# Neighbourhood attention in a two-network kernel: the values' products of two pairs of heads back to back, the context's output products spread, the decay levels one step ahead, own tiles at the end

## The chip, the cores and the metric

The kernel runs on one core of one Trainium2 chip. The metric is the device time of one execution in microseconds (us); lower is better. The kernel before took 1268.24 us, the median of three runs (1267.25 to 1268.48).

The engines are named as in the profile: PE is the matrix engine (TensorE; PEld its loading of weights), DVE the vector engine, ACT the scalar engine, POOL GpSimd, and SP the engine that starts most DMA transfers. PE reads its operands from SBUF and writes into PSUM, which has eight banks here; DVE and ACT read the products from there. Each engine runs its own instructions in the order in which they were written for it, and waits at a semaphore when an operand, or the place for a result, isn't there yet.

## The reference, cut to what matters

Two blocks of layers follow each other on 256 tokens of 1024 numbers. Everything is float32.

```python
def gla_mixer(h, w_in, w_gk_up, b_gk, g_onorm, w_out):      # gated linear attention
    proj = h @ w_in                                          # q, k, v, r, gk_low
    log_a = log_sigmoid(gk_low @ w_gk_up + b_gk) / 16
    ...
    # per chunk of 64 tokens, b = cumsum(log_a):
    decay = exp(where(causal, b_i - b_j, -inf))
    attn = einsum('bhik,bhjk,bhijk->bhij', qb, kb, decay)
    state = state * exp(b_last) + k_dec.T @ vb
    ...
    return (rms_norm(o, g_onorm) * silu(r)) @ w_out

x = x + gla_mixer(rms_norm(x, ...), ...)
x = x + sqrelu_mlp(rms_norm(x, ...), w1, w2)
x = rms_norm(x, final_norm)
# second block: 256 latent tokens (h) and 256 context tokens (hc)
# layer 0, neighbourhood attention: 16 heads of 64, a window of 8 rows x 16 columns, bias rpb
y_lat = softmax([q k_nb * scale + bias, q k_ctx * scale]) @ [v_nb, v_ctx] @ w_o
y_ctx = softmax(q_ctx k_ctx * scale) @ v_ctx @ w_o
# then a SwiGLU FFN on both, grouped-query attention with rotary angles, a second FFN
return rms_norm_2(h, norm_final)
```

## The kernel before, in words

One function, `net`, writes the whole program. A float32 product is made of three products of a narrower float type (`mm3`, lines 178 to 180): high part times high part, low times high, and high times low. So every weight tile of 128 x 1024 that SP loads (`w_load`, line 150) is split by ACT into a high part `wh` (line 161) and by DVE into the rest `wl` (line 162). `wnext` hands out the tiles in one fixed order (`UNITS`) and splits a few ahead (`cap`). The tiles `wh` and `wl` lie in a ring of 12; the probabilities of the neighbourhood attention use the same ring.

The order of the instructions of PE, POOL and SP, and of DVE in most places, comes from a scheduler that works at build time on the program as it is written; ACT's order is the written one in the parts below, and at the end DVE's as well (`manual_schedule`). All 8 PSUM banks are tiles of one pool.

**Gated linear attention (lines 425 to 680).** Eight units `f` make q and k, transposed. Then a loop over `k` makes the values `v`: 12 products of 512 columns for each `k` (two tiles of tokens, two halves, three products; `mm_r`). Two sets of gate products (`gate_half`) follow. Beside them the matrix of decayed scores is built by levels. `decay_sums(t)` (line 431) makes the cumulated log decay of token tile `t` with four products against a triangle, and ACT copies it out (line 433). Then there are nine generators, `core`: `level_diag` (products line 488, masked by DVE on line 490), seven times `level` (subtractions by DVE on lines 501 and 502, exponentials by ACT on line 504, multiplications by DVE on lines 507 and 508, then eight products on PE, line 522, or line 516 for the last level, and a masked copy by DVE, line 528), and `level_cross` (products line 545). `core_step()` runs the products of the generator that stands open and opens the next one, which writes its part on DVE and ACT up to the products. It is called once after each `k`. So a level's DVE work is written one `k` ahead of its products.

`heads_out` and `gated_heads` (line 621) make the outputs of the heads, `heads_T(ks)` transposes them (PE line 630; ACT copies the high part, line 633, DVE makes the low part, line 634). The loop over `w_out` (line 662) does three of its eight `k` for both token tiles, and keeps the last five in `late`; these follow tile by tile, so that the first token tile is done early. Ahead of the last unit of the second tile, `to_T` (line 217) transposes the first tile for the next layer: eight transposes, evacuated by ACT (line 224) and DVE (line 225).

**Neighbourhood attention (lines 821 to 1059).** There are eight pairs of heads, and for each pair six units of work (two heads, and for each the context's queries and two tiles of latent queries). `staged` starts a unit per step and moves every unit that is under way by one stage: scores on PE (lines 891 and 892, 922 and 923), the maximum on DVE, the exponential on ACT (lines 900, 932 and 933), the division on DVE (lines 905 and 937), four transposes on PE (lines 911 and 941), the copy by ACT (lines 915 and 945). In each step `fill(n)` puts some of the generator `steps` between them: the projections of the next pairs (`na_proj`; ACT lines 862 to 878, DVE lines 864 to 876), and at the end the context's output products (`oproj_ctx`, 16 steps of three products). After the last unit of a pair, `done` hands over `na_pv` (line 948), the products of probabilities and values: 24 products into one bank (line 957), those of the two heads side by side in halves of the array; in the step after that ACT copies (line 963) and DVE subtracts (line 964) to make `oT`, which the output products read.

**The end (lines 1493 to 1543).** The last products come in three pieces: 512 columns, 256 and 256. After each, DVE adds the residual (lines 1499 and 1500), ACT squares and sums (line 1502), and DVE multiplies by the gain (line 1535), in place, so behind ACT's reading of the same tile. Then DVE adds the sums (line 1536), POOL makes the root (line 1538), ACT scales the second half (line 1539) and DVE the first (line 1541), and two DMAs write them out.

## Time and profile before

| | before |
|---|---|
| median of three runs | 1268.24 us |
| the profiled execution: its own time | 1267.33 us |
| its span in the trace | 1265.5 us |
| granted clock of PE | 0.998 |
| PE busy | 1249.0 us, 99% of the span |
| DVE busy | 920.0 us, 73% |
| ACT busy | 686.1 us, 54% |
| POOL busy | 79.2 us, 6% |
| DMA, mean rate | 183 GB/s |

The span is the time from the first to the last instruction of the profiled execution; its own time holds the starting and ending around that. Rows of the timeline give the start in us, the duration in us, engine, line, operation, and the names of what is written and read; a number in square brackets is the time for which the engine stood idle before the row, with the instruction whose end it waited for. The matrix engine works in a pipeline, so a product's duration is longer than the distance to the next one's start. That distance, from start to start, tells what a product costs PE.

### The profile page before, as it was taken

What the parts mean: (1) busy time and instruction counts of PE and PEld (TensorE: products, weight loads), DVE (VectorE), ACT (ScalarE), POOL (GpSimd) and SP (SyncE); (2) the same over time, 40 slices, a digit from 0 to 9 for tenths busy, and PEclk for the clock granted to TensorE, in tenths of its full rate; (3) what the DMA queues carried; (4) which work ended last, traced back from release to release, by engine and by line L of the source; (5) the groups of instructions that cost most, each with busy time, mean ns of one, the idle gap of its engine ahead of it and who ended that gap; (6) DMA issues with size and microseconds to landing.
All of it is one profiled execution on the core that took longest, in us unless ns stands there. A gap on an engine that the chain in (4) does not pass through costs nothing.

```text
span 1265.5 us, 18648 instructions
## 1 busy us (share of the span) xinstructions
PE 1249.0 (99%) x6874; PEld 1043.6 (82%) x6874; DVE 920.0 (73%) x1629; ACT 686.1 (54%) x1335; POOL 79.2 (6%) x139
## 2 busy tenths in 40 slices
PE   9999999999999999999999999999999999999997
PEld 8878898988888777789888888888888677899996
DVE  5868788797988888777877667623668888655555
ACT  7565655666548888754332122323457797644443
POOL 1000000030100000001000000000002320000000
PEclk9999999999999999999999999999999999999999
DMA  8646587877572334463656777633664224665650
GB/s 302 202 133 212 190 293 255 283 267 260 183 251 98 126 114 114 155 197 114 210 184 204 248 258 252 219 100 102 198 200 117 67 84 128 215 190 184 187 180 34
DMA packets 68507, 231.22 MB, mean 183 GB/s; under 512 B 8048, under 2 KB 8736, under 8 KB 68416
## 3 DMA queue, kind: packets, MB, share of 16 engines
q1 hardware_dynamic: 68128, 229.68, 56.0%
q8 instruction: 54, 0.88, 0.3%
q10 hardware_dynamic: 288, 0.35, 0.1%
q14 instruction: 37, 0.30, 0.1%
HBM read 228.93 MB, written 1.07 MB: 182 GB/s over the span
## 4 chain that ended last, share of the span: by engine, by line
PE 84%; DVE 7%; ACT 6%; issue 1%; DMA 1%; POOL 0%; POOLq 0%; SPq 0%; DVEq 0%; ACTq 0%
PE b L178 26%; PE b L179 25%; PE b L180 25%; DVE wl L162 2%; PE b L1420 1%; ACT wh L161 1%; PE b L217 1%; PE b L1406 1%; PE b L522 1%; DMA raw<-in_wst_dram 1%; DVE a L309 1%; ACT t L878 1%; DVE t L309 1%; PE b L1387 0%; PE b L957 0%
## 5 line engine op out<-in xcount | busy, mean ns | idle before, releaser
L161 ACT CAST wh<-raw 128x1024 fp32r<-128x1024 f32 x310 | 322.8, 1044 | 391.2 <-PE b L179 295.7
L162 DVE TENSOR_TENSOR wl<-raw,wh 128x1024 fp32r<-128x1024 f32 x310 | 375.0, 1215 | 157.7 <-ACT wh L161 154.0
L179 PE MATMUL b<-t,wl 128*128 128x256 f32 (+1 forms) x1120 | 365.8, 327 | 0.3 <-DVE wl L162 0.3
L178 PE MATMUL b<-t,wh 128*128 128x256 f32 (+1 forms) x1120 | 366.1, 327 | 0.0
L180 PE MATMUL b<-t,wh 128*128 128x256 f32 (+1 forms) x1120 | 365.3, 327 | 0.0
L178 PE MATMUL b<-wh,t 128*128 128x512 f32 (+1 forms) x748 | 298.2, 401 | 1.2 <-ACT t L235 0.6
L180 PE MATMUL b<-wl,t 128*128 128x512 f32 (+1 forms) x748 | 295.1, 395 | 0.0
L179 PE MATMUL b<-wh,t 128*128 128x512 f32 (+1 forms) x748 | 294.9, 394 | 0.1
L179 PEld LDWEIGHTS b<-t,wl 128*128 128x128 f32 x1120 | 210.8, 188 | 22.6 <-DVE wl L162 0.6
L178 PEld LDWEIGHTS b<-t,wh 128*128 128x128 f32 x1120 | 210.7, 188 | 22.3 <-issue 0.2
L180 PEld LDWEIGHTS b<-t,wh 128*128 128x128 f32 x1120 | 210.5, 188 | 20.6 <-DVE t L236 0.2
L180 PEld LDWEIGHTS b<-wl,t 128*128 128x128 f32 x748 | 140.5, 188 | 33.7
L178 PEld LDWEIGHTS b<-wh,t 128*128 128x128 f32 x748 | 140.4, 188 | 32.6 <-ACT t L235 1.0
L179 PEld LDWEIGHTS b<-wh,t 128*128 128x128 f32 x748 | 140.8, 188 | 31.0 <-DVE t L634 0.6
L309 DVE CUSTOM_DVE_ANT_0 a<-a,crow 128x1024 f32<-128x1024 f32 x96 | 117.0, 1226 | 28.3 <-DMA a<-in_ada_dram 27.7
L309 DVE CUSTOM_DVE_ANT_0 t<-a,crow 128x1024 bf16<-128x1024 f32 x64 | 78.5, 1236 | 8.8 <-DMA a<-in_ada_dram 8.8
L1065 DVE TENSOR_TENSOR t<-b,t 128x512 f32<-128x512 f32 (+1 forms) x42 | 23.6, 563 | 59.4 <-PE b L180 52.2
L190 POOL TENSOR_TENSOR c<-c,mhalf 128x1 f32<-128x1 f32 x21 | 14.2, 674 | 537.7 <-DVE c L189 537.6
L324 POOL TENSOR_TENSOR mod<-mod,bcol 128x8 f32<-128x8 f32 x20 | 14.4, 719 | 478.3 <-DVE mod L309 476.0
L1071 ACT CAST t<-t 128x512 fp32r<-128x512 f32 (+1 forms) x42 | 21.7, 517 | 34.6 <-DVE t L1065 34.6
L197 ACT ACTIVATE t<-t 128x512 f32<-128x512 f32 x40 | 24.8, 624 | 10.8 <-DVE t L1034 6.4
L1396 ACT ACTIVATE t<-b,c,c 128x512 f32<-128x512 f32 x32 | 25.9, 811 | 3.4 <-POOL c L1394 3.4
(239 smaller groups left out, 1201.4 us busy)
## 6 DMA issues: line engine op xcount, KB each, us to landing
raw<-in_wst_dram SPq DMA_DIRECT2D x310, 512.0 KB, 4.4
a<-in_ada_dram SPq DMA_DIRECT2D x96, 512.0 KB, 4.4
t<-in_rpb_dram SPq DMA_DIRECT2D x16, 256.0 KB, 4.1
t<-row SPq DMA_DIRECT2D x12, 256.0 KB, 4.9
t<-in_ctx_dram SPq DMA_DIRECT2D x8, 256.0 KB, 5.8
t<-in_xt_dram SPq DMA_DIRECT2D x4, 256.0 KB, 5.9
t<-in_x_dram SPq DMA_DIRECT2D x4, 256.0 KB, 6.3
crow<-in_cvec_dram SPq DMA_DIRECT2D x2, 512.0 KB
```

What stands on the lines that cost most here:

```text
L161: A.copy(out=h[:, :n], in_=raw[:, :n])
L162: V.tensor_tensor(out=l[:, :n], in0=raw[:, :n], in1=h[:, :n], op=ALU.subtract)
L178: T.matmul(o, lhsT=lh, rhs=rh, start=first, stop=False)
L179: T.matmul(o, lhsT=ll, rhs=rh, start=False, stop=False)
L180: T.matmul(o, lhsT=lh, rhs=rl, start=False, stop=last)
L190: G.tensor_tensor(out=ms[:, 3:4], in0=ms[:, 2:3], in1=mhalf[:, 0:1], op=ALU.pow)
L197: A.activation(out=junk[hf], in_=halves[hf], func=AF.Square, scale=1.0 / 32.0, accum_out=ms[:, hf:hf + 1])
L309: V.tensor_tensor_reduce(out=raw if ci == n_c - 1 else t2([D], BF16), in0=raw, in1=crow[ci], scale=1.0, scalar=0.0, op0=ALU.mult, op1=ALU.add,
L324: G.tensor_tensor(out=m, in0=m, in1=bcol[:, L, v, :], op=ALU.add)
L1065: V.tensor_tensor(out=a, in0=pg_[:, :n], in1=a, op=ALU.mult)
L1071: A.copy(out=h, in_=a)
L1396: A.activation(out=pl, in_=sl, func=AF.Exp, scale=r, bias=mx[:, 1:2], accum_out=mx[:, 2:3])
```

## The change

It has five parts.

1. `decay_sums(0)` and `decay_sums(1)` come after units 6 and 7 of the `f` loop (before: after unit 7, and after `k` = 0 of the value loop). `level_diag` and the first `level` are opened ahead of the value loop, so two generators stand open all the time: a level's products come one `k` earlier, and its DVE work is written two `k` ahead of them.
2. The `w_out` loop does four `k` at once and keeps four (before: three and five). Transposes 4 and 5 of `heads_T` come after `k` = 1, 6 and 7 after `k` = 2 (before: all four after the loop).
3. The eight transposes of the first token tile come in three lots, 2, 3 and 3, around the last three units of the second tile (before: all eight ahead of the last unit).
4. `na_pv` takes a list of pairs. Pairs (0, 1), (2, 3) and (4, 5) have their products done one group after the other, each group in its own bank; pairs 6 and 7 stay alone. From unit 40 on `fill` takes one and two steps in turn, up to unit 52 (before: two, up to unit 47).
5. At the end the products with the gain go to tiles of their own, `ys_`; the product of the first half with the gain moves ahead of the last piece; and the last DVE instruction is a product with one scalar (before: with the scalar and with the gain).

```diff
-        if f == 7:
-            decay_sums(0)
+        if f > 5:
+            decay_sums(f - 6)
...
+    for _ in range(2):
+        open_.append(core.pop(0))
+        run(open_[-1])
...
-        if k == 0:
-            decay_sums(1)
...
-        if k < KD - 5:
+        if k < KD - 4:
             for t in range(NT):
                 mm_r(ac[t], u, yT[k], t, k == 0, False)
         else:
             late.append((k, u))
-    heads_T(range(4, KD))
+        if k in (1, 2):
+            heads_T((2 * k + 2, 2 * k + 3))
     hT = new_T()
+    first_T = to_T_steps([xin[0]], hT, 0, vc[:, V_FFN0, :])
     for t in range(NT):
         for k, u in late:
-            if (t, k) == (1, KD - 1):
-                to_T([xin[0]], hT, 0, vc[:, V_FFN0, :])
+            if t == 1 and k > KD - 4:
+                run(first_T, k - KD + 5)
             mm_r(ac[t], u, yT[k], t, False, k == KD - 1)
         residual(xin[t], ac[t])
+    run(first_T, KD)
...
-    def na_pv(pr):
-        po = bank()
+    def na_pv(prs):
+
+        pos = []
+        for pr in prs:
+            po = bank()
...
+            pos.append(po)
+        yield
+        for pr, po in zip(prs, pos):
+            oT[pr] = (t2([N2], F32R), t2([N2], F32R))
+            A.copy(out=oT[pr][0], in_=po)
+            V.tensor_tensor(out=oT[pr][1], in0=po, in1=oT[pr][0], op=ALU.subtract)
...
     def fill(n):
-        if n < len(order):
-            run(steps, (n + 1) * 16 // 6 - n * 16 // 6 if n < 40 else 2)
+        if n < len(order) + 5:
+            run(steps, (n + 1) * 16 // 6 - n * 16 // 6 if n < 40 else 1 + n % 2)
...
     def done(m):
         pr, r = divmod(m, 6)
-        return [na_pv(pr)] if r == 5 else []
+        if r < 5 or pr in (0, 2, 4):
+            return []
+        return [na_pv((pr - 1, pr) if pr < 6 else (pr,))]
...
-    ms, zs_ = col(), [t2([512]) for _ in range(2)]
+    ms, zs_, ys_ = col(), [t2([512]) for _ in range(2)], [t2([512]) for _ in range(2)]
...
-        if n > 0:
-            V.tensor_tensor(out=zs_[1][:, lo:lo + w], in0=zs_[1][:, lo:lo + w], in1=nfb[1][:, lo:lo + w], op=ALU.mult)
+        for y, z, g in ((ys_[1][:, lo:lo + w], zs_[1][:, lo:lo + w], nfb[1][:, lo:lo + w]), (ys_[0], zs_[0], nfb[0]))[:(0, 2, 1)[n]]:
+            V.tensor_tensor(out=y, in0=z, in1=g, op=ALU.mult)
...
-    A.activation(out=zs_[1], in_=zs_[1], func=AF.Copy, scale=r)
-    out_rows(nc.scalar, 1, 512, zs_[1])
-    V.scalar_tensor_tensor(out=zs_[0], in0=zs_[0], scalar=r, in1=nfb[0], op0=ALU.mult, op1=ALU.mult)
-    out_rows(nc.sync, 1, 0, zs_[0])
+    A.activation(out=ys_[1], in_=ys_[1], func=AF.Copy, scale=r)
+    out_rows(nc.scalar, 1, 512, ys_[1])
+    V.tensor_scalar(out=ys_[0], in0=ys_[0], scalar1=r, scalar2=None, op0=ALU.mult)
+    out_rows(nc.sync, 1, 0, ys_[0])
```

Where the scheduler puts this shows in the order of the instructions. On PE, at the end of the value loop, the kernel before has the products of the fifth and sixth level (tiles `t_744` and `t_748`, `t_782` and `t_786`) with one product of the weight stream between them; the rows ahead are products of 512 columns.

```order
L178 MATMUL b_514<-wh_632,t_124 128x512
L179 MATMUL b_514<-wh_632,t_124 128x512
L522 MATMUL b_770<-t_744 128x128 x2
L522 MATMUL b_776<-t_744 128x128 x2
L522 MATMUL b_770<-t_748 128x128 x2
L522 MATMUL b_776<-t_748 128x128 x2
L180 MATMUL b_514<-wl_633,t_124 128x512
L522 MATMUL b_806<-t_782 128x128 x2
L522 MATMUL b_813<-t_782 128x128
L522 MATMUL b_806<-t_786 128x128 x2
L522 MATMUL b_813<-t_782 128x128
L522 MATMUL b_813<-t_786 128x128 x2
```

The kernel after has the sixth level's products (tiles `t_738` and `t_742`) behind a whole `k` of the weight stream, 12 products; these are the last seven of them, and the first of the next `k`.

```order
L180 MATMUL b_531<-wl_620,t_123 128x512
L178 MATMUL b_532<-wh_620,t_123 128x512
L179 MATMUL b_532<-wh_620,t_123 128x512
L180 MATMUL b_532<-wl_620,t_123 128x512
L178 MATMUL b_533<-wh_620,t_123 128x512
L179 MATMUL b_533<-wh_620,t_123 128x512
L180 MATMUL b_533<-wl_620,t_123 128x512
L522 MATMUL b_806<-t_738 128x128 x2
L522 MATMUL b_806<-t_742 128x128 x2
L522 MATMUL b_813<-t_738 128x128 x2
L522 MATMUL b_813<-t_742 128x128 x2
L178 MATMUL b_530<-wh_668,t_124 128x512
```

Before, 14 products of the stream stood between the groups of most levels, and one between the last two; after, there are 12 between every two of the six groups, ahead of the first and behind the last.

On PE in the neighbourhood attention, the kernel before goes from a pair's last product with the values (bank `b_4244`) to the next unit's scores (line 922) and the projection of a later pair.

```order
L957 MATMUL b_4244<-p_4091,t_3449 64x256
L957 MATMUL b_4244<-p_4194,t_3449 64x256
L957 MATMUL b_4244<-p_4091,t_3451 64x256
L957 MATMUL b_4244<-p_4194,t_3451 64x256
L922 MATMUL b_4257<-t_3862,t_3860 128x512
L923 MATMUL b_4257<-t_3864,t_3860 128x512
```

The kernel after goes from the same products (line 965 there) to those of the next pair, in the bank `b_4474`.

```order
L965 MATMUL b_4461<-p_4091,t_3449 64x256
L965 MATMUL b_4461<-p_4194,t_3449 64x256
L965 MATMUL b_4461<-p_4091,t_3451 64x256
L965 MATMUL b_4461<-p_4194,t_3451 64x256
L965 MATMUL b_4474<-t_4272,t_3449 64x256
L965 MATMUL b_4474<-t_4380,t_3449 64x256
```

The first of the two groups has moved behind the whole of the next pair; the number of products is the same.

On DVE, the last rows of the kernel before are these; `t_12430` is the second half of the last token tile, `t_12429` the first.

```order
L1499 TENSOR_TENSOR t_12430<-b_12449,t_10540 128x256
L1500 TENSOR_TENSOR t_12430<-t_12430,t_80 128x256
L1535 TENSOR_TENSOR t_12430<-t_12430,t_10543 128x256
L1499 TENSOR_TENSOR t_12430<-b_12469,t_10540 128x256
L1500 TENSOR_TENSOR t_12430<-t_12430,t_80 128x256
L1531 SCALAR_TENSOR_TENSOR c_12428<-c_12428 128x1
L1535 TENSOR_TENSOR t_12430<-t_12430,t_10543 128x256
L1536 TENSOR_TENSOR c_12428<-c_12428 128x1
L1541 SCALAR_TENSOR_TENSOR t_12429<-t_12429,c_12428,t_10542 128x512
```

And these those of the kernel after, whose line numbers are 12 higher.

```order
L1511 TENSOR_TENSOR t_12430<-b_12451,t_10540 128x256
L1512 TENSOR_TENSOR t_12430<-t_12430,t_80 128x256
L1547 TENSOR_TENSOR t_12432<-t_12430,t_10543 128x256
L1547 TENSOR_TENSOR t_12431<-t_12429,t_10542 128x512
L1511 TENSOR_TENSOR t_12430<-b_12472,t_10540 128x256
L1512 TENSOR_TENSOR t_12430<-t_12430,t_80 128x256
L1543 SCALAR_TENSOR_TENSOR c_12428<-c_12428 128x1
L1547 TENSOR_TENSOR t_12432<-t_12430,t_10543 128x256
L1548 TENSOR_TENSOR c_12428<-c_12428 128x1
L1553 TENSOR_SCALAR t_12431<-t_12431,c_12428 128x512
```

One DVE instruction of 512 columns is new, ahead of the last piece, and the products with the gain write `t_12431` and `t_12432`, which ACT's squares don't read.

25 lines of the change are left out of this document (11 added, 14 removed).

## The prediction

> **What bounds the kernel now.** I read the page first, then the list of what PE waited for, then the timeline around those waits, and the table of stretches for the attention.
>
> ```profile
> PE 1249.0 (99%) x6874; PEld 1043.6 (82%) x6874; DVE 920.0 (73%) x1629; ACT 686.1 (54%) x1335; POOL 79.2 (6%) x139
> ```
>
> ```profile
> PE b L522 <- DVE t L508: 1.6, 1, 1.6
> ```
>
> PE is busy for 1249.0 of 1265.5 us, so PE's queue is the path, and nothing here removes a product: the gain can only be time in which PE stands, or goes slower than its pace. The list of waits has one long one, 1.6 us at the levels. Since idle time counts from modelled ends, I go by distances from start to start. The next rows are the timeline: PE, ACT and DVE at the levels, then a stretch of the attention that waits for nothing.
>
> ```profile
> 41.86 1.95 PE L488 MATMUL b<-t,t 128*128 128x128 f32 x16
> ...
> 52.16 1.95 PE L522 MATMUL b<-t 128*128 128x128 f32 x16
> ...
> 57.21 1.95 PE L522 MATMUL b<-t 128*128 128x128 f32 x16
> ...
> 69.25 0.47 PE L180 MATMUL b<-wl,t 128*128 128x512 f32 x1
> 71.28 2.02 PE L522 MATMUL b<-t 128*128 128x128 f32 x16 [1.55 <-DVE t L508]
> ...
> 39.26 0.65 ACT L433 COPY t<-b 128x256 f32<-128x256 f32 x2 [1.38 <-PE b L431]
> ...
> 40.87 1.28 ACT L504 ACT_TABLE_LOAD   x1
> ...
> 44.45 0.42 DVE L501 TENSOR_TENSOR t<-t 128x256 f32<-128x256 f32 x1
> ...
> 47.81 1.22 DVE L162 TENSOR_TENSOR wl<-raw,wh 128x1024 fp32r<-128x1024 f32 x1
> 48.94 1.35 DVE L528 COPY_PREDICATED t<-masks,b 128x512 f32<-128x512 uint8 x2
> ...
> 54.00 1.34 DVE L528 COPY_PREDICATED t<-masks,b 128x512 f32<-128x512 uint8 x2
> ...
> 520.27 0.60 PE L911 MATMUL b<-cm,t 128*128 128x128 f32 x4
> 520.63 0.48 PE L178 MATMUL b<-wh,t 128*128 128x512 f32 x1
> 520.95 0.40 PE L179 MATMUL b<-wh,t 128*128 128x512 f32 x1
> 521.18 0.39 PE L180 MATMUL b<-wl,t 128*128 128x512 f32 x1
> ```
>
> The last four rows give the pace: four transposes 0.36, a product of 512 columns behind them 0.32, any other 0.23. DVE's masked copies stand 5.06 apart: that is its round for a level. At 69.25 one product takes 2.03 us.
>
> **Part 1, the levels.** The product at 69.25 should take 0.32, so the wait costs 1.7. What comes in its place? With 12 products between groups instead of 14, PE's round is 5.05 (52.16 to 57.21) less 2 x 0.23 = 4.6; DVE's stays 5.06, so DVE loses 0.5 per level and needs a lead at the start. It gets one: with both sums ahead of the value loop ACT's copies end near 37.1 (39.26 + 0.65 less one `k` of 12 x 0.23 = 2.8), and the first subtraction comes near 36.9 instead of 44.45, no longer behind line 490. From there to the masked copy it was 4.5 us (44.45 to 48.94); the table load, now in the way until 38.4, adds 0.5: 41.9. Then come two maskings (1.2, as line 528) and the second level's arithmetic, a round less masking and split (5.06 - 1.2 - 1.1 = 2.8), and one subtraction more, 0.3: its factors are there at 46.2, and the later levels' 5.06 apart. PE has line 488 at 41.86 - 2.8 = 39.05, the first level 4.6 later, and wants the second's at 48.2. So the lead is 2.0, then 1.5, 1.1, 0.6, 0.1 and about nothing for line 516. I charge 0.1 there: **1.6** (0.9 to 1.8).
>
> **Parts 2 and 3, transposes.** In the timeline of PE:
>
> ```profile
> 118.42 0.40 PE L178 MATMUL b<-wh,t 128*128 128x512 f32 x1
> 118.95 0.50 PE L179 MATMUL b<-wh,t 128*128 128x512 f32 x1
> ...
> 127.87 0.40 PE L180 MATMUL b<-wl,t 128*128 128x512 f32 x1
> 128.64 0.58 PE L217 MATMUL b<-cm,t 128*128 128x128 f32 x2 [0.37 <-DVE t L225]
> 129.16 0.51 PE L178 MATMUL b<-wh,t 128*128 128x512 f32 x1
> ```
>
> At 118.42 a product takes 0.53 instead of 0.23; it stands for DVE's low part of a head's transpose. Transposed one or two `k` earlier, the heads are ready in time; late next is line 621, whose result the new place wants about when it is there: **0.3** (0 to 0.4). At 127.87 the eight transposes run out of banks: 0.77 - 0.23 = 0.54, then 0.52 for two transposes worth 0.2. In lots of 2, 3, 3 with six products between, a lot's evacuations fit between lots: **0.85** (0.5 to 1.0). No load on SP's queue is moved past a wait here; ACT's weight casts stay among the evacuations.
>
> **Part 4, the values' products.** PE again, around one group and around the late places:
>
> ```profile
> 421.42 0.60 PE L911 MATMUL b<-cm,t 128*128 128x128 f32 x4
> 421.95 1.08 PE L957 MATMUL b<-t,t 128*64 128x256 f32 x8
> ...
> 424.69 0.50 PE L922 MATMUL b<-t,t 128*128 128x512 f32 x1
> 425.03 0.39 PE L923 MATMUL b<-t,t 128*128 128x512 f32 x1
> ...
> 504.62 0.47 PE L178 MATMUL b<-wh,t 128*128 128x512 f32 x1
> 505.29 0.38 PE L891 MATMUL b<-t,t 128*128 128x256 f32 x1 [0.19 <-ACT t L900]
> ...
> 521.88 0.39 PE L180 MATMUL b<-wl,t 128*128 128x512 f32 x1
> 522.64 0.63 PE L941 MATMUL b<-cm,t 128*128 128x128 f32 x4 [0.36 <-ACT t L933]
> ...
> 523.58 0.63 PE L941 MATMUL b<-cm,t 128*128 128x128 f32 x4 [0.31 <-ACT t L915]
> ```
>
> Four transposes, the group and the next product take 0.53 + 2.74 + 0.34 = 3.61 (421.42 to 425.03); without the group, 0.68 (520.27 to 520.95). So a group alone costs 2.93. The second of a double group costs its body, 2.74, or some 0.1 less where its first and last pair lose what they lose now by the switch. Three merges at 0.2 to 0.33: **0.9** (0 to 1.0), the low end if the 0.17 on entry is a wait for the probabilities. The Trainium skill speaks to that: "TensorEngine Tiling (Array Packing)", section "Key Properties", says that changing the tiling mode drains the engine. By that rule each merge saves two switches, and the sum stays as it is; without it, it would be 0.5 to 0.9 smaller.
>
> At 504.62 a product takes 0.67 instead of 0.32, since line 891 waits for ACT; ACT has a double group's time there now: **0.35** (0 to 0.35). In the tail, 0.76 instead of 0.23 at 521.88, and 0.94 at 522.64 for four transposes worth 0.4: 1.05 in all. The spread output products go between. I leave 0.2: **0.85** (0.3 to 1.0).
>
> What the merge costs is seen in the table of stretches, one pair each (length, then busy PE, PEld, DVE, ACT), and in the timeline of the second pair.
>
> ```profile
> 402.35:421.95 19.60, 19.60 (x114) 15.49 (x113) 17.29 (x50) 16.27 (x45) 0.00 (x0) 1.00 0.34 111
> 421.95:441.53 19.58, 19.58 (x114) 15.49 (x113) 16.84 (x49) 16.30 (x44) 0.00 (x0) 1.00 0.35 109
> ```
>
> ```profile
> 412.68 0.49 DVE L937 TENSOR_SCALAR t<-t,c 128x512 f32<-128x512 f32 x1
> ...
> 416.11 0.60 PE L941 MATMUL b<-cm,t 128*128 128x128 f32 x4
> ```
>
> A pair without its group is 19.6 - 2.74 = 16.8 us of PE. DVE's 16.84 to 17.29, less 0.7 for line 964, are 16.1 to 16.6: it keeps up only if nearly all its idle time goes. DVE's division ends 2.9 us ahead of its transposes (413.17, 416.11), so a later short pair may lose 2.7 without harm. The first may not: its lead is the 2.74 of the group at 402.35, which goes. I charge 0.4 there, once (0 to 1.5).
>
> **Part 5, the end.** DVE's and ACT's last rows:
>
> ```profile
> 1256.64 0.42 DVE L1500 TENSOR_TENSOR t<-t,t 128x256 f32<-128x256 f32 x1
> ...
> 1258.03 0.42 DVE L1535 TENSOR_TENSOR t<-t,t 128x256 f32<-128x256 f32 x1 [0.97 <-ACT t L1502]
> 1258.38 0.41 DVE L1499 TENSOR_TENSOR t<-b,t 128x256 f32<-128x256 f32 x1
> ...
> 1259.61 0.19 ACT L1502 ACTIVATION_READ_ACCUMULATOR t<-t 128x1 f32 x1
> ...
> 1260.17 0.15 DVE L1536 TENSOR_TENSOR c<-c 128x1 f32<-128x1 f32 x1
> ```
>
> The product with the gain waits 0.97 for ACT, and line 1499 of the last piece stands behind it. Without the wait DVE goes on at 1257.06 with 0.35 for that product and some 0.55 for the new one of 512 columns, and line 1499 starts near 1257.96, 0.42 earlier. Line 1536 then follows ACT's sum at once (1259.80 - 0.42 = 1259.4) and not a product later: **0.76** (0.6 to 0.9). The shorter last instruction lies beside ACT's scaling and its DMA: nothing.
>
> **Sum.** 1.6 + 0.3 + 0.85 + 0.9 + 0.35 + 0.85 + 0.76 = 5.6; less 0.4 for the first short pair and 0.2 for new waits of a tenth each: 5.0. The profiled execution's own time, 1267.33, is 0.9 under the median of 1268.24, within the runs' spread, so the sum is taken from the median: **1263.2 us**, and a profiled execution near 1262.3.
>
> **The rivals.**
>
> *The short pairs are DVE's.* For: 16.1 to 16.6 against 16.8, and ACT and DVE answer each other several times in a unit. Against: the later pairs' leads. If the first loses 1.5 and the other two 0.4 each, 1.9 more than I charged goes: 1265.1. Chance 0.15.
>
> *The pairs keep 19.6 us, and the merge is a loss.* If scores, maximum, exponential, division and copies need 19.6 with the group or without, short pairs save nothing and the second groups come on top: 3 x 2.7 = 8.1 against 4.7 of other gains, **1271.6 us**. It decides when DVE and ACT have over 2.7 us in a pair in which neither can go on; that PE waits nowhere in the middle pairs speaks against it. Chance 0.04. The Trainium skill has a rule that bears on its price: "TensorE: Matmul & The Clock Gate", Part 3, lets products in different columns of the array run together, some 4 ns apart; by that a group would take about 1.4 us (an estimate from 12 pairs of 256 columns at 2.4 GHz) and this rival would end near 1267.7. The trace doesn't agree: 24 products take 2.74.
>
> *The levels stay DVE's.* If DVE starts 1 us later than I have it, the lead is gone by the fourth level, and 1.2 of the 1.6 comes back: 1264.4. Chance 0.10.
>
> *The early gains are given back.* If DVE's weight splits don't move forward with PE, parts 1 to 3 are swallowed at the next `w_out` unit: 5.0 - 2.75 = 2.25, 1266.0. For it: DVE has little idle time at the levels; against: these splits wait for ring places that PE sets free. Chance 0.06.
>
> **How the numbers follow.** My case has 0.65. With the upper ends of its terms it reaches 6.4, and the runs spread by 0.4 on their medians: low 1261.4. Up to 1266.0 the range takes in the first, third and fourth rival and leaves out the slower one. A measurement of this kernel tells about 0.2%, 2.5 us, from no change, so faster means below 1265.7: my case, the third rival, most of the first, and some doubt for all of them, 0.86; same 0.10; slower 0.04.
>
> **What would show it.** Right: no wait over 0.3 at line 522; three double groups of line 957 about 5.4 us long, with one entry of 0.17 each; nothing over 0.4 at the other places named; line 1536 within 0.1 of ACT's last sum. Wrong: waits of over 1 us at transposes in the pair ahead of the first double group; pairs without a group longer than 17.2 us; a level's wait over 0.8.

## The result, and the profile after

| | before | after |
|---|---|---|
| median | 1267.42 us (six runs, 1266.69 to 1268.48) | 1260.95 us (six runs, 1260.72 to 1261.89) |
| profiled execution, its own time | 1267.33 us | 1260.8 us |
| its span | 1265.5 us | 1259.0 us |

The ratio of after to before is 0.9949, with a 95% interval of 0.9937 to 0.9962: 6.5 us faster, where 5.0 were forecast. The median of 1260.95 us lies 0.45 below the low end of the range. The sign held, and the mechanism at most of the places; sizes and the base did not. The forecast of 1263.2 is 2.25 too high: 0.8 is its base, since three more runs moved the median of before from 1268.24 to 1267.42, and 1.4 is the gain. The first row of the page after:

```profile
PE 1245.7 (99%) x6874; PEld 1043.8 (83%) x6874; DVE 918.4 (73%) x1630; ACT 686.6 (55%) x1335; POOL 80.3 (6%) x139
```

As many products as before, and still 99%: what went is time in which PE stood or went slower than its pace. (From the attention on, lines have other numbers in after: 916 and 946 are the transposes, 911 and 941 in before; 927 and 928 the scores, 922 and 923; 965 the values' products, 957; 1547, 1548 and 1553 at the end, 1535, 1536 and 1541.)

**The lead.** The way to place the gain is PE's lead: the start of one and the same product, in before and in the other kernel, subtracted. A change of the lead between two products that have the same work between them is time gained or lost there. In us, at the time that the product has in before:

| | 31 | 82, behind the levels | 130, behind the transposes | 391, in the first pairs | 553, behind the attention | 1100 | 1256, last products | span |
|---|---|---|---|---|---|---|---|---|
| after | -0.1 | 1.9 | 3.3 | 3.6 | 5.3 | 5.5 | 5.5 | 6.5 |

So 2.0 us come from the levels, 1.4 from the stretch of the transposes, 0.3 near 374 us, 1.8 from the attention, 0.2 behind it and 1.0 from the end. Of the 1.4, about 0.4 belong to this one execution of before (see the transposes below).

**The levels.** PE's rows after, the groups from the diagonal (line 488) to the last level (line 516):

```profile
39.12 1.95 PE L488 MATMUL b<-t,t 128*128 128x128 f32 x16
...
43.71 1.95 PE L522 MATMUL b<-t 128*128 128x128 f32 x16
...
66.64 1.95 PE L522 MATMUL b<-t 128*128 128x128 f32 x16
...
71.32 1.15 PE L516 MATMUL b<-t 128*64 128x64 f32 x16
```

The first distance is 4.59, the 4.6 that was worked out, and so are the five from 43.71 to 66.64 (43.71 + 5 x 4.59 = 66.66); no row has a wait. Only the last distance, 4.68, is a tenth longer. The list of what PE waited for has no line 522 any more.

**The transposes of the first tile**, PE after:

```profile
120.94 0.38 PE L217 MATMUL b<-cm,t 128*128 128x128 f32 x2
121.08 0.48 PE L178 MATMUL b<-wh,t 128*128 128x512 f32 x1
...
122.56 0.49 PE L217 MATMUL b<-cm,t 128*128 128x128 f32 x3
122.81 0.47 PE L178 MATMUL b<-wh,t 128*128 128x512 f32 x1
```

Two transposes take 0.14 (120.94 to 121.08) and three 0.25; before, the last two took 0.52, and the product ahead of them 0.77. In lead, this part gives 0.95 (2.31 to 3.26; in e11 0.29 to 1.24, in r3 0.25 to 1.20).

The other 0.4 of this stretch come at the place that the prediction named for part 2, the product at 118.42 in before, which took 0.53. The experiments r1 (the kernel before once more), e1, e7 and e8 have that code unchanged, and gain 0.3 to 0.4 on before at the same place; in r1 the product takes 0.24 (118.87 to 119.11). What differs is a load. ACT's rows, of before and then of r1:

```profile
116.25 1.05 ACT L161 CAST wh<-raw 128x1024 fp32r<-128x1024 f32 x1 [0.57 <-DMA raw<-in_wst_dram]
```

```profile
116.15 1.05 ACT L161 CAST wh<-raw 128x1024 fp32r<-128x1024 f32 x1
```

In before this cast waits 0.57 for its weights; DVE's split of them waits for the cast, and the low part of the transpose (line 634) stands behind the split. So part 2 is not shown to gain anything.

**A double group**, PE after, from the transposes ahead of it (line 916) to the scores behind it:

```profile
414.91 0.60 PE L916 MATMUL b<-cm,t 128*128 128x128 f32 x4
415.44 1.08 PE L965 MATMUL b<-t,t 128*64 128x256 f32 x8
...
418.08 1.03 PE L965 MATMUL b<-t,t 128*64 128x256 f32 x8
...
420.77 0.50 PE L927 MATMUL b<-t,t 128*128 128x512 f32 x1
421.11 0.39 PE L928 MATMUL b<-t,t 128*128 128x512 f32 x1
```

From 415.44 to 420.77 it is 5.33 us: 2.64 for the first 24 products and 2.69 for the second. There is one entry, 0.53 for four transposes worth 0.36, and one exit, 0.34 for a product worth 0.23. The 24 products of 2.64 us also show again that the two halves of the array don't run together here: the estimate of 1.4, from the Trainium skill's "TensorE: Matmul & The Clock Gate", Part 3, doesn't hold in this kernel.

The table of stretches for the 39.16 us from this double group to the next (length, then busy PE, PEld, DVE, ACT):

```profile
415.44:454.60 39.16, 39.16 (x229) 31.30 (x230) 33.78 (x101) 33.22 (x88) 0.00 (x0) 1.00 0.36 110
```

5.33 for the double leave 33.83 for two pairs, or 16.9 each: the 16.8 of the prediction, with DVE busy for 33.78 of 39.16.

**The tail of the attention**, PE after:

```profile
509.84 2.18 PE L965 MATMUL b<-p,t 128*64 128x256 f32 x16
511.95 0.50 PE L927 MATMUL b<-t,t 128*128 128x512 f32 x1
...
517.32 0.60 PE L946 MATMUL b<-cm,t 128*128 128x128 f32 x4
518.28 0.63 PE L946 MATMUL b<-cm,t 128*128 128x128 f32 x4 [0.35 <-DVE t L942]
518.83 1.08 PE L965 MATMUL b<-t,t 128*64 128x256 f32 x8
...
520.27 0.49 PE L178 MATMUL b<-wh,t 128*128 128x512 f32 x1
...
522.57 0.51 PE L179 MATMUL b<-wh,t 128*128 128x512 f32 x1
```

The four transposes at 517.32 still take 0.96, 0.6 more than the 0.36 they are worth; before, the two places took 1.05 too much. So 0.45 is gained and 0.6 is left. Two more costs stand in these rows: the 16 products at 509.84 take 2.11, where the same ones took 1.83 in before (517.01 to 518.84), which is a new loss of 0.28; and a product of line 178 has been put inside the last group, which is so in before as well.

**The end**, DVE and ACT after:

```profile
1253.44 0.42 ACT L1514 ACTIVATE t<-t 128x256 f32<-128x256 f32 x1 [0.34 <-DVE t L1512]
1253.44 0.43 DVE L1547 TENSOR_TENSOR t<-t,t 128x256 f32<-128x256 f32 x1
1253.76 0.18 ACT L1514 ACTIVATION_READ_ACCUMULATOR t<-t 128x1 f32 x1
1253.98 0.16 DVE L1548 TENSOR_TENSOR c<-c 128x1 f32<-128x1 f32 x1
...
1254.79 0.48 DVE L1553 TENSOR_SCALAR t<-t,c 128x512 f32<-128x512 f32 x1 [0.66 <-POOL c L1550]
```

The product with the gain (line 1547) runs beside ACT's square, and the sum (line 1548) starts 0.04 behind ACT's last row: as foreseen. The last instruction takes 0.48 instead of 0.75.

### The profile page after: what moved, and what is told of

It is laid out like the page before. It is cut to its first block, busy times and chain, and to the rows that moved or that the text cites. A ratio compares the mean times of both kernels' runs of the same rounds, so it can differ in the third digit from the quotient of the medians.

```text
span 1259.0 us, 18654 instructions
## 1 busy us (share of the span) xinstructions
PE 1245.7 (99%) x6874; PEld 1043.8 (83%) x6874; DVE 918.4 (73%) x1630; ACT 686.6 (55%) x1335; POOL 80.3 (6%) x139
## 4 chain that ended last, share of the span: by engine, by line
PE 95%; ACT 2%; DVE 2%; issue 1%; DMA 0%; POOL 0%; POOLq 0%; SPq 0%
PE b L178 28%; PE b L179 28%; PE b L180 28%; PE b L965 2%; PE b L1432 1%; PE b L946 1%; PE b L217 1%; PE b L1418 1%; PE b L522 1%; PE b L927 1%; PE b L928 1%; DVE wl L162 1%; PE b L916 1%; PE b L1399 0%; ACT wh L161 0%
```

## The experiments

My theory was the prediction's: the gain is waits at PE and switches of PE's mode. The first rivals were that the merge of pairs is worth nothing or a loss, and that DVE is near its limit in the short pairs. The leads of the runs, as in the table above (minus: behind the kernel before):

| lead of PE, us | 31 | 82 | 130 | 391 | 553 | 1100 | 1256 | span |
|---|---|---|---|---|---|---|---|---|
| e1_levels_only | 0.0 | 1.9 | 2.4 | 2.7 | 2.6 | 2.8 | 1.9 | 1.9 |
| e2_one_ahead | 0.0 | -0.9 | 0.5 | 0.7 | 2.4 | 2.5 | 1.6 | 2.5 |
| e3_dve_late | 0.2 | 1.2 | 2.6 | 2.9 | 4.6 | 4.7 | 4.7 | 5.6 |
| e4_pairs_alone | -0.5 | 1.5 | 2.9 | 3.2 | 3.4 | 3.6 | 2.7 | 3.7 |
| e5_step_between | 0.2 | 2.2 | 3.6 | 3.6 | -1.3 | -1.2 | -1.2 | -0.3 |
| e6_dve_load_after | 0.0 | 2.0 | 3.4 | 3.1 | 3.5 | 3.6 | 2.7 | 3.7 |
| e10_all_doubles | 0.0 | 2.0 | 3.4 | 3.7 | 4.4 | 4.5 | 3.6 | 4.6 |
| e11_transposes_only | 0.0 | -0.1 | 1.2 | 0.2 | 0.1 | 0.2 | -0.7 | -0.7 |
| e12_steps_later | 0.0 | 2.0 | 3.4 | 3.3 | 6.3 | 6.5 | 6.5 | 7.4 |
| r1_before_again | -0.4 | -0.4 | -0.1 | -0.3 | -0.3 | -0.2 | -0.2 | -0.3 |
| r2_after_again | -0.1 | 1.8 | 3.2 | 3.5 | 5.2 | 5.5 | 4.6 | 5.6 |
| r3_transposes_again | -0.1 | -0.1 | 1.2 | 0.8 | 0.8 | 0.9 | 0.0 | 0.0 |

Some runs lose 0.9 between 1100 and 1256 us, r2 among them, which is the kernel after once more. That is no effect of an edit; the last section has it.

**e1_levels_only**: before, with part 1 alone.

> The kernel before with the first part alone: both sums in the f loop, two generators open ahead of the value loop. My theory: the whole gain of the levels is the one wait at line 522, so PE is 1.7 to 1.95 us ahead of the kernel before from the gate products on, keeps that to the end, and the time is 1.6 to 2.2 us shorter. Rival (gains upstream are given back): PE is ahead behind the levels, and the lead is gone by the w_out units or the first pair of heads, the time within 0.5 us of the kernel before.

Measured: 1265.44 us, ratio 0.9983 (0.9973 to 0.9993). The lead goes from -0.02 to 1.93 at the levels: 1.95, as in after. That gain doesn't need the other parts.

**e2_one_ahead**: after, with one generator opened ahead.

```diff
-    for _ in range(2):
+    for _ in range(1):
```

> The kernel after with the two sums early as there, but only one generator opened ahead of the value loop, so a level's DVE work is written one k ahead of its products and not two. Theory of DVE's lead: the first subtraction stands behind line 490 again, DVE's round is 5.06 us and PE's again about 5.05 with 14 products between groups, so nothing is gained on the way, and the last two groups (lines 522 and 516) come with no product between them, for a wait of 1.2 us, between 0.8 and 2.0, in the levels. Rival (early sums are what counts): no wait over 0.3 us there, and the levels as in the kernel after.

Measured: 1264.75 us, one run. The round is 5.05 again and the wait is back, at the last level and longer than I expected. PE:

```profile
49.39 1.95 PE L522 MATMUL b<-t 128*128 128x128 f32 x16
54.44 1.95 PE L522 MATMUL b<-t 128*128 128x128 f32 x16
...
69.60 1.95 PE L522 MATMUL b<-t 128*128 128x128 f32 x16
73.79 0.65 PE L516 MATMUL b<-t 128*64 128x64 f32 x8 [2.24 <-DVE t L508]
```

With one generator the earlier sums give nothing at the levels (the lead there falls to -0.9); the second generator on top of them, that is the work written two `k` ahead, gives 2.8 us. The second generator without the earlier sums was not tried. DVE's rows say why, of e2 and then of after:

```profile
40.16 0.69 DVE L490 TENSOR_TENSOR t<-b,cm 128x512 f32<-128x512 f32 x1 [1.93 <-PE b L488]
...
41.67 0.42 DVE L501 TENSOR_TENSOR t<-t 128x256 f32<-128x256 f32 x1
```

```profile
36.92 0.42 DVE L501 TENSOR_TENSOR t<-t 128x256 f32<-128x256 f32 x1 [0.37 <-ACT t L433]
```

With one generator open, the first subtraction (line 501) is queued behind the masking of the diagonal, and DVE stands 1.93 us for PE; with two, it starts 4.75 us earlier, and the level's work fills that idle time.

**e3_dve_late**: after, with two more DVE instructions in the second level, whose result nobody uses.

```diff
+        if li == 2:
+            spare = t2([512])
+            for n in range(2):
+                V.tensor_tensor(out=spare, in0=zs[0], in1=zs[1], op=ALU.add)
```

> The kernel after with two more DVE instructions of 512 columns, 1.25 us, ahead of the third level; their result isn't used. Theory: DVE has no idle time from there to the last level, and the trace of after has the last factors 0.2 to 0.3 us ahead of PE (lines 522 and 516), so PE waits for 0.9 us, 0.7 to 1.2, at the last three levels. If DVE has room that the durations don't show, PE waits for less than 0.3.

Measured: 1261.65 us, one run; the levels give 1.0 instead of 1.95. Two instructions cost PE 0.9: the lead that part 1 gives DVE is small at its end, as worked out, and the rival "the levels stay DVE's" was near.

**e4_pairs_alone**: after, with every pair's group by itself.

```diff
-        if r < 5 or pr in (0, 2, 4):
-            return []
-        return [na_pv((pr - 1, pr) if pr < 6 else (pr,))]
+        return [na_pv((pr,))] if r == 5 else []
```

> The kernel after with every pair's products with the values in a group of their own again, and all else as after, the spread output products too. If the merge saves the price of switching (my theory, 0.33 us a merge) and the late product at line 891 (0.35), this takes 1.0 to 1.4 us longer than the kernel after. If the gain in the attention came from the spread output products and not from the merge, it takes 0.3 us longer at most.

Measured: 1263.40 us, ratio 0.9966 (0.9953 to 0.9979). The attention gains 0.2 instead of 1.76, so the merge is worth 1.56, and "the merge is a loss" falls. It is more than the switches (1.0, next experiment). Two waits make most of the rest: the 16 products of pair 6 take 2.44 here (2.11 in after), and one product near 507 us takes 0.16 too much.

**e5_step_between**: after, with a step of three products between the two groups of a double.

```diff
         for pr in prs:
+            if pos:
+                run(steps, 1)
             po = bank()
```

> The kernel after with one step of the projections, three products of 512 columns, between the two groups of each double where steps are left. No group moves to another pair and no product is added. If the saving is the price of a switch into the halved array and out of it, each such double costs 0.33 us more, 0.6 to 1.0 us in all, seen as 0.5 from transposes or products to the group and 0.34 behind it. If the entry was a wait for the probabilities, the second group enters without loss, since its probabilities have long been there, and the span stays within 0.2 us, but for the tail, where the steps taken earlier are missing.

Measured: 1267.59 us, one run. PE at the first double:

```profile
414.89 0.60 PE L916 MATMUL b<-cm,t 128*128 128x128 f32 x4
...
418.16 0.50 PE L178 MATMUL b<-t,wh 128*128 128x512 f32 x1
...
419.05 1.08 PE L967 MATMUL b<-t,t 128*64 128x256 f32 x8
...
422.13 0.40 PE L928 MATMUL b<-t,t 128*128 128x512 f32 x1
```

From 414.89 to 422.13 it is 7.24; in after, from 414.91 to 421.11, 6.20. Three products at 0.23 are 0.70, so leaving the mode and coming back costs 0.34 here, and 0.32 by the leads; at the second double the leads give 0.67 for both, the same price again. That is the price of a switch, for which the Trainium skill's "TensorEngine Tiling (Array Packing)", section "Key Properties", has the rule without a figure; the trace agrees with the rule. But the attention as a whole is 6.65 us worse than in after (the lead goes from 3.6 to -1.3, and not from 3.55 to 5.3), of which the two switches are 0.67. I had not expected the other 6. They come behind the second double. A row of DVE, one of PE, and the stretch behind that (length, then busy PE, PEld, DVE, ACT, POOL, and the granted clock of PE):

```profile
466.56 1.23 DVE L162 TENSOR_TENSOR wl<-raw,wh 128x1024 fp32r<-128x1024 f32 x1 [3.46 <-ACT wh L161]
...
494.12 0.63 PE L946 MATMUL b<-cm,t 128*128 128x128 f32 x4 [2.25 <-DVE c L940]
```

```profile
494.80:498.20 3.40, 3.40 (x13) 2.87 (x12) 1.68 (x6) 3.34 (x7) 0.00 (x0) 0.50 0.14 51
```

Three times between 470 and 495 us PE waits for DVE's division, 4.0 us in all. It isn't for want of products between: ahead of the two long waits stand 12 products of the projections each, against 9 and 11 at the same places in after. DVE itself is late. The moved step changes the order that the scheduler gives DVE: ahead of the first long wait a weight split (line 162) stands ahead of the next unit's maximum, where it stands behind it in after, and it waits 3.46 us for ACT; ahead of the second, DVE works from 484 us on with hardly a stand. Behind the longest wait the granted clock is 0.50 for 3.4 us, and a product of 512 columns takes 0.43 instead of 0.23: about 1.6 us more. The rest, some 0.4, is not placed; part of it is at the tail, where the steps used earlier are missing. So e5 gives the price of a switch, and its 6 us are another thing: an order of DVE's work in which its chain isn't hidden.

**e6_dve_load_after, e7_dve_load_before**: one more maximum by DVE per latent unit, in after and in before; its result isn't used.

```diff
         V.tensor_reduce(out=mx[:, 1:2], in_=sl[:, S:N2], axis=AX.X, op=ALU.max)
+        V.tensor_reduce(out=mx[:, 3:4], in_=sl[:, S:N2], axis=AX.X, op=ALU.max)
```

> The kernel after with one more DVE maximum over 256 columns in each latent unit of the attention, four a pair, 1.4 us a pair; its result isn't used. My account that a pair without its group of products is nearly all DVE's: the division ends 0.4 us ahead of its transposes in the short pairs of after, so the three short pairs lose 0.7 to 1.4 us each, 2 to 4 us in all, in waits at the transposes, and the double groups hide the load in the others. If the leads of later short pairs were 2.7 us as I had forecast, only the first would lose.

> The same more DVE instructions in the kernel before, 1.4 us a pair. A pair there has 2.7 us in which DVE does nothing, and the transposes come 2.9 us behind the division: the load is hidden from the second pair on, and the attention takes 0 to 0.8 us longer, in the first pair and in the tail. If DVE set the pace of the pairs of before already, it would take 5 us and more.

Measured: 1263.59 and 1268.25 us, one run each. In after the attention gives 0.4 instead of 1.76: the load costs 1.4, less than expected. In before it costs nothing (0.44 behind at 391 us, 0.35 at 523), as expected. So DVE is near its limit in the short pairs and was not before, which is the first rival's mechanism; only the limit isn't reached.

**e8_end_only**: before, with part 5 alone.

> The kernel before with the fifth part alone, own tiles, the early product and the shorter last instruction. My sum had 0.76 us for it, from the wait at line 1535; the trace of the kernel after has 1.1 from the last pieces on. If 0.86 is the wait and 0.25 the shorter last instruction (its DMA starts earlier beside ACT's), the span is 1.0 to 1.2 us shorter; if the 0.25 was chance, 0.7 to 0.9.

Measured: 1266.64 us, ratio 0.9992 (0.9982 to 1.0001), which by itself is no difference. In the trace the last products come 0.73 later than in before and the span is 0.28 shorter (1265.26 against 1265.53), so the end gives 1.0.

**e9_long_last**: after, with the last DVE instruction as in before; the product moved ahead stays, and its result isn't used.

```diff
-    V.tensor_scalar(out=ys_[0], in0=ys_[0], scalar1=r, scalar2=None, op0=ALU.mult)
-    out_rows(nc.sync, 1, 0, ys_[0])
+    V.scalar_tensor_tensor(out=zs_[0], in0=zs_[0], scalar=r, in1=nfb[0], op0=ALU.mult, op1=ALU.mult)
+    out_rows(nc.sync, 1, 0, zs_[0])
```

> The kernel after with its last DVE instruction long again, with the scalar and the gain, from the tile without the gain; the early product is still made, and not used. If the 0.2 to 0.25 us between the last DMA's issue and the end come from SP's transfer of the first half starting 0.26 earlier beside ACT's, the distance from ACT's last issue to the end of the span is 3.7 us again as in the kernel before (3.46 in after). If that is chance, it stays at 3.5.

Measured: 1261.45 us, one run. DVE's last row:

```profile
1255.16 0.75 DVE L1553 SCALAR_TENSOR_TENSOR t<-t,c,t 128x512 f32<-128x512 f32 x1 [0.66 <-POOL c L1550]
```

The two output DMAs start behind the last instructions of ACT (second half) and DVE (first half; SP issues that DMA). The times of the issues and of the end of the span, in us:

| | ACT's issue | SP's issue | end | end less ACT's issue | end less SP's issue |
|---|---|---|---|---|---|
| before | 1261.79 | 1261.82 | 1265.53 | 3.74 | 3.72 |
| after | 1255.54 | 1255.31 | 1259.02 | 3.48 | 3.72 |
| e8 | 1261.79 | 1261.55 | 1265.26 | 3.47 | 3.71 |
| e9 | 1255.91 | 1255.94 | 1259.67 | 3.75 | 3.73 |

With the long instruction the end comes 0.27 later behind ACT's issue, as expected. The last column says more: in all 17 traces the end comes 3.65 to 3.73 behind SP's issue, while behind ACT's it is 3.46 to 3.48 with the short instruction and 3.68 to 3.75 with the long one. So the end follows DVE's last instruction and SP's DMA, and not ACT's, which starts up to 0.24 later.

**e11_transposes_only**: before, with parts 2 and 3 alone.

> The kernel before with the second and third part alone, the transposes in lots and one unit fewer kept back. My terms are 0.3 and 0.85, the trace of after has 1.34 for both: PE gains 1.0 to 1.4 us between the gate products and the next layer, and keeps it. If the earlier place needs the lead of the levels, which isn't there in this kernel, PE waits at line 630 and the gain is under 0.7.

Measured: 1268.02 us, one run. The lead grows by 1.3 at the transposes without the levels' lead (0.4 of it is what r1 shows too). Then the lead loses 1.1 near 374 us, at the first pair of heads. PE there, and DVE ahead of it:

```profile
373.58 0.39 PE L895 MATMUL b<-t,t 128*128 128x256 f32 x1 [1.09 <-ACT t L881]
```

```profile
366.82 1.23 DVE L309 CUSTOM_DVE_ANT_0 t<-a,crow 128x1024 bf16<-128x1024 f32 x1 [2.34 <-DMA a<-in_ada_dram]
```

DVE's share of the copies of q and k (line 867, 864 in before) is queued behind line 309, which waits 2.34 us for a load. The first scores need those copies; the experiments r1 to r3 come back to this place.

**e10_all_doubles**: after, with pairs 6 and 7 as a double too.

```diff
-        if r < 5 or pr in (0, 2, 4):
-            return []
-        return [na_pv((pr - 1, pr) if pr < 6 else (pr,))]
+        return [na_pv((pr - 1, pr))] if r == 5 and pr % 2 else []
```

> The kernel after with the last two pairs' products back to back as well. A fourth merge saves 0.33 us by the price of the switch. But PE comes to the last units' transposes 2.7 us earlier, with no group of the seventh pair and none of its output products before them, and the leads there are 0.1 to 0.3 us: DVE sets the end of the attention, PE waits 1.5 to 3 us at the transposes, and the kernel is 1 to 2.5 us slower than after. If the tail had room, it is 0.3 faster.

Measured: 1263.34 us, ratio 0.9970 (0.9960 to 0.9979). The attention gives 0.7, 1.0 less than in after. PE at the tail:

```profile
515.88 0.63 PE L946 MATMUL b<-cm,t 128*128 128x128 f32 x4 [1.86 <-DVE t L942]
```

A switch is saved, worth 0.33, but pair 6's group was the cover of pair 7's last divisions.

**e12_steps_later**: after, with the output products spread further.

```diff
-            run(steps, (n + 1) * 16 // 6 - n * 16 // 6 if n < 40 else 1 + n % 2)
+            run(steps, (n + 1) * 16 // 6 - n * 16 // 6 if n < 40 else 1 + (n % 3 == 0))
```

> The kernel after with the context's output products spread further to the back, one step and every third time two, so that one step stands between the last two groups of transposes. The tail of after still has 0.8 us too much there, a wait of 0.5 for the last division and 0.28 within the last single group but one. If these waits are for want of something to do, PE gains 0.4 to 0.8 us; if DVE and ACT end the tail, which start no earlier, the steps taken from the units ahead open waits there, and the sum is within 0.3 us of after.

Measured: 1260.21 us (1259.85 to 1260.46), ratio 0.9946 (0.9929 to 0.9963), the fastest version; before took 1267.08 beside it. Against after the ratios' intervals overlap; by the traces its attention gives 3.0 instead of 1.76. PE at the tail:

```profile
509.55 1.90 PE L965 MATMUL b<-p,t 128*64 128x256 f32 x16
511.38 0.50 PE L927 MATMUL b<-t,t 128*128 128x512 f32 x1
...
517.88 0.60 PE L946 MATMUL b<-cm,t 128*128 128x128 f32 x4
518.41 1.08 PE L965 MATMUL b<-t,t 128*64 128x256 f32 x8
...
521.67 0.39 PE L179 MATMUL b<-wh,t 128*128 128x512 f32 x1
```

All three remaining costs of after's tail go: the 16 products take 1.83 instead of 2.11, the transposes don't wait (0.6), and no product stands inside the last group. That group and the product take 3.26 (518.41 to 521.67) instead of 3.74 (518.83 to 522.57). These make 0.28 + 0.6 + 0.48 = 1.4, of which 1.2 shows in the lead.

**r1_before_again, r2_after_again, r3_transposes_again**: before, after and e11 unchanged, to see what belongs to the execution.

> The kernel before once more, for a second look at two places that the change doesn't touch: the first pair's copies near 373 us (PE stood 0.29 us there in before, 1.1 to 1.4 in three variants of it, none in after) and the products of 256 columns in the last feed-forward part (117.3 ns from start to start in some traces, 118.7 in others, 0.9 us in all). If these are a matter of the execution, one of them at least comes out differently from the first look: a stand of 0.6 or more, or 118.7. If they belong to the kernel, both repeat.

> The kernel after once more. The same two places: if they belong to the execution, the stand at the first pair may be anything up to 0.5, and the products in the last part 117.3 or 118.7; if to the kernel, none and 117.3. The stages that the change touches repeat within 0.1 us: levels 1.95, transposes 1.4, attention 1.76, end 1.0 against the kernel before.

> The kernel before with the second and third part alone, once more. In the first look PE was 1.3 us ahead behind the transposes and lost 1.07 of it at the first pair of heads, where DVE's share of the copies stood behind an instruction that waited 2.34 us for a transfer. If that transfer's landing is a matter of the execution, the loss is another one now (less than 0.7, or more than 1.4); if early gains are swallowed there as a rule, it is 0.9 to 1.3 again.

Measured: 1267.57, 1261.72 and 1267.31 us, one run each. r2 agrees with after within 0.1 up to 1100 us. At the first pair PE stands 0.3 in before and 0.5 in r1, 1.4 in e11 and 0.7 in r3, and 0 to 0.05 in after and r2. So that place differs between executions of one kernel. The wait that matters there is line 309's for its load. The lead ahead of the first pair, the time by which that instruction starts earlier than in before (366.99 us there), and the lead behind the pair:

| | lead at 360 us | line 309 earlier by | lead at 391 us |
|---|---|---|---|
| after | 3.26 | 3.69 | 3.55 |
| r2_after_again | 3.24 | 3.49 | 3.48 |
| e12_steps_later | 3.37 | 3.33 | 3.31 |
| e11_transposes_only | 1.24 | 0.17 | 0.16 |
| r3_transposes_again | 1.20 | 0.83 | 0.81 |
| r1_before_again | -0.06 | -0.26 | -0.28 |
| e8_end_only | -0.03 | -0.64 | -0.66 |
| e7_dve_load_before | 0.42 | -0.43 | -0.44 |

In all 17 traces the lead behind the pair is, within 0.02, the smaller of two numbers: the lead ahead of it plus 0.29, which is before's own stand, and the time by which line 309 starts earlier. So in before and its variants without part 1 the landing of that load sets when PE goes on, and what PE gained ahead of it is lost unless the load lands earlier too. With part 1 and two generators it lands 2.9 to 3.8 us earlier, and most or all of the lead passes; why it lands so much earlier there was not followed.

## Why the prediction was right or wrong

**Right**: what bounds the kernel, four of the five parts and their direction; no rival took over in after.

**What failed** is the sum and the base under it. Three of its terms were mis-sized: the shorter last instruction, put at nothing, is worth 0.25; the levels, put at 1.6, gave 1.95; and the 0.4 charged to the first short pair is 0. And the sum was taken from a median of 1268.24, where six runs give 1267.42.

| step | predicted | measured |
|---|---|---|
| levels | 1.6 | 1.95 |
| transposes of the heads (part 2) | 0.3 | 0.4, of which nothing is shown to be the edit's |
| transposes of the first tile (part 3) | 0.85 | 0.95 |
| merges | 0.9 | 1.0 for three switches |
| line 891 | 0.35 | 0.35 (505.19 to 505.55, no wait) |
| tail | 0.85 | 0.45 |
| first short pair | -0.4 | 0 |
| small new waits | -0.2 | -0.28 at the 16 products of pair 6; 0.1 at line 516 is within the 1.95 |
| end, up to ACT's last issue | 0.76 | 0.74 |
| shorter last instruction | 0 | 0.25 to 0.27 |
| first pair, near 374 us | - | 0.3 |

The measured terms make 6.1. To that come 0.2 behind the attention and 0.1 lost at the start, neither of which the change touches, and 0.3 that no row was found for, most of it in the attention: 6.5.

- **Levels.** Right in mechanism, 0.35 short. The product at 69.25 was one of three places where before lost time. PE before, at the other two:

```profile
46.68 0.39 PE L179 MATMUL b<-wh,t 128*128 128x512 f32 x1
47.03 2.02 PE L522 MATMUL b<-t 128*128 128x128 f32 x16
...
63.08 0.48 PE L180 MATMUL b<-wl,t 128*128 128x512 f32 x1
63.40 1.05 PE L522 MATMUL b<-t 128*128 128x128 f32 x8
```

  A product of 0.35 instead of 0.23 (46.68 to 47.03), and a group cut in two by a product of 0.32 instead of 0.23: 0.2 that I had not counted. After has neither. The other 0.15 was not placed in full; a group of line 545 near 81 us, cut in two in before and whole in after, makes 0.1 of it. The charge of 0.1 for the last level was right in size (4.68 instead of 4.58).
- **Part 2's 0.3** has the right size by luck. The prediction read the slow product at 118.42 as the cost of transposing late; r1 has the same code and no such product, so it was the wait of one execution for a load of weights. Against r1 the stretch of the transposes gives 1.0 in r2, all of it part 3.
- **"I charge 0.4 there, once"** failed: in after the pair ahead of the first double loses nothing, and the two short pairs take 16.9 each. The lead of 2.74 that I took from the first was not needed. e6 shows that the reserve is small: one instruction more per latent unit cost 1.4 in all.
- **Line 891** was right in size and wrong in reason: "ACT has a double group's time there now". In e4, which has no double groups, its wait is gone as well, so it is the spread of the steps that takes it.
- **The tail** failed the other way: "the spread output products go between. I leave 0.2". 0.6 was left at the last transposes, because one and two steps in turn still leave nothing to put ahead of the last transposes. e12 gains it with fewer steps per turn. Of what the prediction named as signs, this is the only one that came out wrong: over 0.4 at a named place.
- **"The shorter last instruction lies beside ACT's scaling and its DMA: nothing"** failed. e9 and the traces give it 0.25 to 0.27. The step took ACT's half for the one that ends last; the end follows SP's DMA of DVE's half, 3.65 to 3.73 behind its issue in every trace. Why it does so in after as well, where SP's DMA is issued first, was not tried.
- **The range.** "With the upper ends of its terms it reaches 6.4, and the runs spread by 0.4" failed twice. The upper ends held no gain at the last instruction, none at the first pair of heads and none of the 0.2 above, which make 0.75 together; and the base was a median of three runs, 0.8 above that of six. The terms came from the profiled execution, so its own 1267.33 was the base that went with them; from there the forecast would have been 1262.3. Taken from six runs' 1267.42, the same terms give 1262.4 and a low end of 1260.6, and the measured 1260.95 lies inside that: the range was missed by its base, and the forecast by the base and the terms.
- **The fourth rival**, early gains given back, is there in the kernel before with parts 2 and 3 alone, but at the first pair of heads and not at the `w_out` unit, and by a load and not by DVE's weight splits: e11 gave back 1.1 of 1.3, and r3 0.4. After gave back nothing, since with part 1 the load lands earlier (the table at r1 to r3). e7 and e8, which have no gain to give back, lose 0.9 and 0.6 at the same place.
- **The merge is a loss**: fell, with e4. **The short pairs are DVE's**: not so in after, but with little to spare: e6 loses 1.4 to one instruction per latent unit, and e5 4.0 to another order of DVE's work.

## What to carry to other kernels

Compare two traces by the start of the same instruction at a dozen places, not by busy time or by the list of waits: here both showed 99% busy, and the lead showed where each half microsecond went. Put a price on the switch of mode (here 0.33 us) and merge, but keep filling work and one late group for the last units: spreading the filling work further gave 1.2 us (e12), and spending the late group cost 1.0 (e10). Where a scheduler orders the engines, moving one step can change the order on another engine, and cost more than the step (e5). A stand that one trace shows can be a load that was late in that execution: look for it in a second one before it becomes a term of a sum. Take the base of a forecast from the execution whose rows give the terms, and run the kernel before more than three times when 1 us matters.

## What the runs showed of the hardware

- Going out of the mode of half-array products and back costs 0.32 to 0.34 us, measured with three products of 512 columns between (e5, at both doubles).
- After PE had waited 2.25 us in e5, the granted clock was 0.50 for 3.4 us. In after it is 1.00 all through the attention.
- The span ends 3.65 to 3.73 us behind SP's last issue in all 17 traces, whether ACT's DMA is issued 0.03 us earlier or 0.24 later.
- In the last feed-forward part, the products of 256 columns follow each other at one of two distances, and one kernel shows both. PE of after and then of r2, the first of 96 such products and the product behind the last:

```profile
1229.37 0.28 PE L178 MATMUL b<-t,wh 128*128 128x256 f32 x1
...
1240.63 0.39 PE L178 MATMUL b<-wh,t 128*128 128x512 f32 x1
```

```profile
1230.14 0.28 PE L178 MATMUL b<-t,wh 128*128 128x256 f32 x1
...
1241.53 0.40 PE L178 MATMUL b<-wh,t 128*128 128x512 f32 x1
```

  11.26 us are 117.3 ns for each, 11.39 are 118.7; over that part it makes 0.9 us. The granted clock is 1.00 in both. Eight traces show the first (before, after, r1, e3, e5, e8, e9, e12) and nine the second. What decides it stays open.
- A load's landing, and not an instruction of PE, decides up to 1.4 us at the first pair of heads (e11, r3), and 0.3 at the heads' transposes (before and r1). So single executions differ by about 1 us at places that the change doesn't touch, and effects under that were read from the leads and not from the times.
